# A hybrid decoder layer on one Trainium2 core: w_in's blocks scaled in place and split whole, and a memory pool for each pair's right-hand factors

## The chip, the core and the metric

The kernel runs on one core of one Trainium2 chip. The metric is the device time of one execution in microseconds. Below, PE is the matrix engine (TensorE), PEld its weight loads, DVE is VectorE, ACT is ScalarE, POOL is GpSimd, and SP is the queue that issues the DMA transfers.

## What is computed

One layer of a hybrid decoder, for 512 prompt tokens and for 8 samples of 8 tokens (576 columns together), all in fp32. Cut to what matters here:

```python
proj = rmsnorm(x, g_mix) @ w_in          # 2048 -> some 5128 columns
a, b, c, d = four mixers of 512 channels # gated DeltaNet, S5, windowed attention, RG-LRU
x = x + concat(a, b, c, d) @ w_out
x = x + cross_attention(rmsnorm(x, g_cross))
hup = rmsnorm(x, g_ffn) @ w_up           # 2048 -> 11264 columns
u, g = split(causal_conv3(hup))
x = x + (silu(g) * u) @ w_down           # 5632 -> 2048
y = rmsnorm(x, g_final)
```

The outputs are y for both groups and the new caches and states (22 arrays).

## The kernel before

Activations stand with channels on partitions: a chunk of 128 channels by 576 tokens is one tile. Every large product keeps fp32 precision by a split: a factor is cut into a part `hi`, rounded to the type fp32r, and a part `lo`, the rest, also fp32r. Three products (hi times hi, hi times lo, lo times hi) are added up in PSUM.

**Weights.** `block` (lines 114 to 130) loads one block of 512 rows by 256 columns (128 partitions by 1024 elements) into a buffer `raw` with SP, and makes `hi` and `lo` of it. There are two buffers each of `raw`, `hi` and `lo`. Without a gain it is one ACT cast of 1024 elements and one DVE subtraction of 1024 elements (lines 123 and 124). With a gain, as for w_in, whose rows are multiplied by g_mix, it is four pairs, one for each 128 rows: ACT makes hi of 256 elements with the gain as its scale (line 128), and DVE makes lo from raw, gain and hi in a fused operation (line 129). w_in has 80 such blocks. `linear` (line 132) multiplies: 48 matmuls of 288 columns for a block of 256 columns.

**Order.** A scheduler in the framework orders each engine's instructions ahead of time, by priorities that `at(...)` sets ("first", "evac", "weights", "drain", "mix", "side", "fill") and by simulated times. On the chip each engine and the SP queue take their instructions in that order, and wait on semaphores.

**Stages.** First x is transposed by PE into `xh` and `xl` (`first_x`). Then w_in's products run, mixed with the work of the four mixers, then w_out, cross-attention, the up-projection (w_up), the down-projection and the final norm.

**The up-projection.** It has 44 products of 256 columns. The first three are plain (`plain_pair`, line 497): they read the normalised rows in `xn`, four pools of four channel chunks each (hi and lo, 18,432 bytes of a partition in a pool), in the order xn0 to xn3. The other 41 (`up_pair`, line 515) use a scheme with 7 products in place of 8, after Winograd, on 2x2 cuts: each product runs over four stretches of 512 rows, and reads of w_up sums that POOL makes (`S`), and of the activations sums that `ffn_x` (line 464) makes once.

**The right factors.** `ffn_x` does this for a pair q of channel chunks (8 pairs): SP loads the pair from DRAM into `z` (line 481); DVE multiplies it by g_ffn and by the row norm r (line 483, two instructions); DVE makes two differences in `t12` (line 476, four subtractions); `halves` (lines 335 to 337) makes Bh and Bl of z, and Th and Tl of t12, each hi by an ACT cast and each lo by a DVE subtraction. Pairs 0 to 3 lie in one pool `xa`, pairs 4 to 7 in one pool `xb`; a pair takes 16,128 bytes of a partition. `xb` is opened where the four `xn` pools lay, after these are closed. A tile of a new pool waits until the pools that lay at its pool's addresses are no longer in use.

The third plain product's results leave PSUM by six DVE instructions (lines 634, 636 and 637). Below this is called the third evacuation.

Of the kernel before, what the change touches and what calls it, by code (L numbers as in the profile page):

```python
# [7 lines left out]
F32 = mybir.dt.float32  # L8
F32R = mybir.dt.float32r
AF = mybir.ActivationFunctionType  # L10
OP = mybir.AluOpType
# [3 lines left out]
NT = 576  # L15
# [3 lines left out]
class Net:  # L19
# [94 lines left out]
    def block(self, w, k0, nk, c0, ncol, gain=None):  # L114

        nc = self.nc
        with self.at("weights"):
            raw = self.wp.tile([128, nk, ncol], F32, tag="raw", name="raw", bufs=2)
            nc.sync.dma_start(raw, w[128 * k0:128 * (k0 + nk), c0:c0 + ncol].rearrange("(k p) c -> p k c", p=128))
            hi = self.wp.tile([128, nk, ncol], F32R, tag="hi", name="hi")  # L120
            lo = self.wp.tile([128, nk, ncol], F32R, tag="lo", name="lo")
            if gain is None:
                nc.scalar.copy(hi, raw)  # L123
                nc.vector.tensor_tensor(lo, raw, hi, op=OP.subtract)  # L124
            else:
                for k in range(nk):
                    g = gain[:, k0 + k:k0 + k + 1]
                    nc.scalar.activation(hi[:, k], raw[:, k], AF.Copy, scale=g)  # L128
                    nc.vector.scalar_tensor_tensor(lo[:, k], raw[:, k], g, hi[:, k], op0=OP.mult, op1=OP.subtract)  # L129
        return hi, lo  # L130

    def linear(self, xh, xl, w, c0, ncol, done, k0=0, nk=None, gain=None):
# [145 lines left out]
class Post(Net):  # L278
# [185 lines left out]
    def ffn_x(self, xc, fp, qs):  # L464

        nc, z = self.nc, {}

        for q in reversed(qs):
            for i, n in ((0, 3), (1, 4)):
                if i:  # L470

                    z[q] = xc.tile([128, 2, NT], F32, name="z", tag=f"h{q}")
                    self.X[q, 1, 1] = xc.tile([128, n, 288], F32R, name=f"Tl{q}")
                else:
                    self.X[q, 0, 0], self.X[q, 0, 1] = (xc.tile([128, n, 288], F32R, name=f"B{p}{q}") for p in "hl")
        sub = lambda o, x, y: nc.vector.tensor_tensor(o, x, y, op=OP.subtract)
        flat = lambda y: y.rearrange("p a b -> p (a b)")
        for q in qs:
            with self.at("drain"):
                x = z[q]  # L480
                nc.sync.dma_start(x, self.xd[2 * q:2 * q + 2].rearrange("k p t -> p k t"))
                for k in range(2):
                    nc.vector.scalar_tensor_tensor(x[:, k], x[:, k], self.v("g_ffn", 2 * q + k), self.r, op0=OP.mult, op1=OP.mult)
                b11, b12, b21, b22 = (x[:, k, 288 * j:288 * j + 288] for k in range(2) for j in range(2))
                t = [fp.tile([128, 592], F32, name="t12", tag=g, bufs=1)[:, :NT].rearrange("p (a b) -> p a b", a=2) for g in "ts"]
                sub(t[0][:, 0], b12, b11)
                sub(t[0][:, 1], b22, t[0][:, 0])
                sub(t[1][:, 0], b22, b12)
                sub(t[1][:, 1], t[0][:, 1], b21)
                h, l = self.X[q, 0, 0], self.X[q, 0, 1]  # L490
                self.halves(h[:, 0], l[:, 0], b11)
                self.halves(flat(h[:, 1:]), flat(l[:, 1:]), x[:, 1])
                h, l = self.X[q, 1, 0], self.X[q, 1, 1] = xc.tile([128, 4, 288], F32R, name=f"Th{q}", tag=f"h{q}"), self.X[q, 1, 1]
                for i in range(2):
                    self.halves(h[:, 2 * i:2 * i + 2], l[:, 2 * i:2 * i + 2], t[i])

# [1506 lines left out]
class Full(S5):  # L2003
# [45 lines left out]
    def run(self):  # L2049
        tc, nc = self.tc, self.nc  # L2050
        pool = lambda n, **k: tc.tile_pool(name=n, bufs=1, **k)
        R = dict(side="right")
# [3 lines left out]
        with ExitStack() as post, ExitStack() as late, ExitStack() as keep, ExitStack() as dx:  # L2056
# [54 lines left out]
            with ExitStack() as ups:  # L2111
                with ExitStack() as xns:

                    self.xn = [xns.enter_context(pool(f"xn{i}", **R)) for i in (3, 2, 1, 0)][::-1]
                    self.mean = xns.enter_context(pool("mn", **R)).tile([128, 128], F32, name="mean")
                    nc.gpsimd.memset(self.mean, 1.0 / 2048)
                    with pool("cw", **R) as cw:
                        self.banks = (0, 1)
                        with self.at("mix"):
                            self.cross_open(cw)  # L2120
                        self.w_out(2, "g_cross")
                        self.banks = (0, 1, 2, 3)
                        with self.at("mix", (3,)):
                            self.row_rstd()
                        self.cross(cw)
                    with self.at("mix", (2, 3)):
                        for m in range(16):
                            self.square(m)
                        self.row_rstd()
                    late.close()  # L2130
                    self.banks = (3,)
                    f1, fp, xa = (ups.enter_context(pool(n)) for n in ("f1", "fp", "xa"))
                    self.ffn_x(xa, fp, range(4))
                    up = self.ffn_up(fp, f1)
                    next(up)
                    for _ in range(3):
                        up.send(self.plain_pair)
                xb, sp = (ups.enter_context(pool(n, **R)) for n in ("xb", "sp"))
                self.ffn_x(xb, fp, range(4, 8))
                for i in range(3, 44):  # L2140
                    up.send(lambda w, c0, done: self.up_pair(sp, w, c0, done, (3, 2, 0, 1) if i == 43 else (0, 1, 2, 3)))
# [44 lines left out]
```

## Time and profile before

| | |
|---|---|
| median of 3 runs | 3052.51 us (3049.77 to 3057.75) |
| the profiled execution | 3051.51 us |
| its span in the trace | 3049.4 us |
| PE busy | 2906.1 us, 95% |
| PEld busy | 2743.9 us, 90% |
| DVE busy | 2074.2 us, 68% |
| ACT busy | 1134.3 us, 37% |
| POOL busy | 1054.8 us, 35% |
| mean granted TensorE clock | 0.986 of full speed |

The span is what the trace shows from the first to the last instruction; 2.1 us of the execution lie around it. A busy share is an average over all stages. PE's share is high, so a gain can only come from the time in which PE stands idle, or runs at a lower granted clock, in single stages.

### The profile page before, as it was taken

How to read it: one execution, taken by the hardware profiler on the slowest of the kernel's cores; microseconds unless marked ns; L12 is line 12 of the kernel's file. 1: busy time of each engine (PE TensorE's matmuls, PEld its weight loads, DVE VectorE, ACT ScalarE, POOL GpSimd, SP SyncE). 2: the span in 40 equal slices, each digit the busy share in tenths (PEclk: the TensorE clock that was granted, in tenths of full speed). 3: DMA queues.
4: the chain of work that ended last, by engine and by line, in shares of the span. 5: the costliest groups of instructions: out<-in, count | busy, mean ns of one | idle time of the engine just before them, and what ended most of it. 6: DMA issues, size and time to landing. Idle time of an engine off the chain costs nothing. (4 is left out here: it accounts for less than half of the span.)

```text
span 3049.4 us, 53981 instructions
## 1 busy us (share of the span) xinstructions
PE 2906.1 (95%) x21347; PEld 2743.9 (90%) x21347; DVE 2074.2 (68%) x3440; ACT 1134.3 (37%) x2025; POOL 1054.8 (35%) x1181
## 2 busy tenths in 40 slices
PE   8979988998999999998899999999999999999998
PEld 7879987887888879988899999999999999999996
DVE  7866666779567566559788888888888953333334
ACT  5434331353433353325344444444444432212214
POOL 2000322313112000102468888888878810000000
PEclk9999999999999999999999999999999999999999
DMA  5455566545566474234333333333333363323322
GB/s 162 151 160 163 173 183 194 160 131 163 168 212 185 139 217 134 80 119 149 118 96 103 107 103 109 107 109 104 107 99 107 114 202 114 104 94 114 107 90 104
DMA packets 370134, 408.41 MB, mean 134 GB/s; under 512 B 37718, under 2 KB 300716, under 8 KB 369177
## 3 DMA queue, kind: packets, MB, share of 16 engines
q1 hardware_dynamic: 369880, 404.96, 42.9%
q8 instruction: 168, 2.75, 0.4%
q14 instruction: 86, 0.70, 0.1%
HBM read 342.85 MB, written 64.69 MB: 134 GB/s over the span
## 5 line engine op out<-in xcount | busy, mean ns | idle before, releaser
L123 ACT CAST hi<-raw 128x1024 fp32r<-128x1024 f32 x158 | 165.6, 1048 | 487.7 <-PE acc L151 422.7
L151 PE MATMUL acc<-xh,hi 128*128 128x288 f32 x1408 | 319.7, 305 | 11.1 <-DVE nt L1185 10.8
L124 DVE TENSOR_TENSOR lo<-raw,hi 128x1024 fp32r<-128x1024 f32 x158 | 195.8, 1240 | 190.9 <-ACT hi L123 187.1
L151 PE MATMUL acc<-xh,lo 128*128 128x288 f32 x1408 | 316.8, 304 | 2.8 <-DVE lo L129 2.8
L151 PE MATMUL acc<-xl,hi 128*128 128x288 f32 x1408 | 319.3, 304 | 0.0
L337 DVE TENSOR_TENSOR lo<-S,hi 128x1024 fp32r<-128x1024 f32 x164 | 227.8, 1389 | 85.6 <-ACT hi L336 85.6
L151 PE MATMUL acc<-hh,hi 128*128 128x288 f32 x1280 | 275.4, 296 | 3.1 <-DVE xT L294 2.5
L337 DVE TENSOR_TENSOR al<-raw,ah 128x512 fp32r<-128x512 f32 x328 | 267.2, 850 | 15.8 <-ACT ah L336 15.8
L151 PE MATMUL acc<-hh,lo 128*128 128x288 f32 x1280 | 273.8, 295 | 1.1 <-DVE lo L124 1.1
L151 PE MATMUL acc<-hl,hi 128*128 128x288 f32 x1280 | 274.4, 295 | 0.0
L151 PEld LDWEIGHTS acc<-xh,hi 128*128 128x128 f32 x1408 | 231.7, 192 | 22.4 <-issue 17.1
L336 ACT CAST hi<-S 128x1024 fp32r<-128x1024 f32 x164 | 171.8, 1047 | 207.7 <-POOL S L532 172.3
L151 PEld LDWEIGHTS acc<-xl,hi 128*128 128x128 f32 x1408 | 232.8, 192 | 9.8 <-issue 9.1
L151 PEld LDWEIGHTS acc<-xh,lo 128*128 128x128 f32 x1408 | 231.7, 192 | 9.6 <-issue 4.4
L294 DVE TENSOR_TENSOR xT<-acc,xT 128x576 f32<-128x576 f32 x160 | 120.7, 755 | 167.1 <-PE acc L151 165.9
L529 POOL TENSOR_TENSOR S<-raw 128x256 f32<-128x256 f32 x164 | 168.3, 1026 | 152.6 <-DMA raw<-in_w_up 121.5
L128 ACT ACTIVATE hi<-raw,gmix 128x256 fp32r<-128x256 f32 x320 | 136.9, 500 | 207.1 <-PE acc L151 186.7
L151 PEld LDWEIGHTS acc<-hh,hi 128*128 128x128 f32 x1280 | 206.2, 188 | 3.9 <-ACT hi L123 2.4
L151 PEld LDWEIGHTS acc<-hh,lo 128*128 128x128 f32 x1280 | 206.4, 188 | 1.3 <-DVE lo L124 1.3
L151 PEld LDWEIGHTS acc<-hl,hi 128*128 128x128 f32 x1280 | 206.8, 188 | 0.0
L553 PE MATMUL acc<-Bh,ah 128*128 128x288 f32 x656 | 197.0, 300 | 9.8 <-ACT t L558 9.7
L627 DVE SCALAR_TENSOR_TENSOR y<-ub,vec,y 128x592 f32<-128x592 f32 x176 | 179.9, 1043 | 35.2 <-ACT y L625 34.4
(705 smaller groups left out, 8109.8 us busy)
## 6 DMA issues: line engine op xcount, KB each, us to landing
raw<-in_w_up SPq DMA_DIRECT2D x176, 512.0 KB
raw<-in_w_down SPq DMA_DIRECT2D x88, 512.0 KB
raw<-in_w_in SPq DMA_DIRECT2D x80, 512.0 KB
raw<-in_w_out SPq DMA_DIRECT2D x32, 512.0 KB
hx<-t SPq DMA_DIRECT2D x44, 288.0 KB
ht<-hx SPq DMA_DIRECT2D x44, 288.0 KB
old<-in_cache_win_k SPq DMA_DIRECT2D x48, 256.0 KB
old<-in_cache_win_v SPq DMA_DIRECT2D x48, 256.0 KB
```

Source lines behind the costliest of these rows:

```text
L123: nc.scalar.copy(hi, raw)
L124: nc.vector.tensor_tensor(lo, raw, hi, op=OP.subtract)
L128: nc.scalar.activation(hi[:, k], raw[:, k], AF.Copy, scale=g)
L151: nc.tensor.matmul(acc[m][:, 224 + 288 * j:512 + 288 * j], wt[:, k, 128 * m:128 * m + 128], at(x, kb + k)[:, 288 * j:288 * j + 288], start ...
L294: nc.vector.tensor_tensor(x, ps, old, op=OP.add)
L336: self.nc.scalar.copy(hi, src)
L337: self.nc.vector.tensor_tensor(lo, src, hi, op=OP.subtract)
L529: g(S[:, 0], A(2, 1), A(2, 2), op=OP.add)
L553: nc.tensor.matmul(P[name], wt[:, i, q], xx, start=ch == chs[0] and q == 0 and j == 0, stop=ch == chs[3] and q == 1 and j == 2)
L627: nc.vector.scalar_tensor_tensor(y, u[:, k:k + 592], w(k), y, op0=OP.mult, op1=OP.add)
```

## The change

In a block with a gain, ACT first multiplies raw by the gain in place, again by four instructions of 256 elements; then one ACT cast of 1024 elements makes hi, and one DVE subtraction of 1024 elements makes lo. For the right factors, there is one pool for each pair in place of one for four pairs, in the same order, at the same addresses.

```diff
                 for k in range(nk):
-                    g = gain[:, k0 + k:k0 + k + 1]
-                    nc.scalar.activation(hi[:, k], raw[:, k], AF.Copy, scale=g)
-                    nc.vector.scalar_tensor_tensor(lo[:, k], raw[:, k], g, hi[:, k], op0=OP.mult, op1=OP.subtract)
+                    nc.scalar.activation(raw[:, k], raw[:, k], AF.Copy, scale=gain[:, k0 + k:k0 + k + 1])
+                nc.scalar.copy(hi, raw)
+                nc.vector.tensor_tensor(lo, raw, hi, op=OP.subtract)
...
-                    z[q] = xc.tile([128, 2, NT], F32, name="z", tag=f"h{q}")
-                    self.X[q, 1, 1] = xc.tile([128, n, 288], F32R, name=f"Tl{q}")
+                    z[q] = xc[q].tile([128, 2, NT], F32, name="z", tag=f"h{q}")
+                    self.X[q, 1, 1] = xc[q].tile([128, n, 288], F32R, name=f"Tl{q}")
                 else:
-                    self.X[q, 0, 0], self.X[q, 0, 1] = (xc.tile([128, n, 288], F32R, name=f"B{p}{q}") for p in "hl")
+                    self.X[q, 0, 0], self.X[q, 0, 1] = (xc[q].tile([128, n, 288], F32R, name=f"B{p}{q}") for p in "hl")
...
-                    f1, fp, xa = (ups.enter_context(pool(n)) for n in ("f1", "fp", "xa"))
+                    f1, fp = (ups.enter_context(pool(n)) for n in ("f1", "fp"))
+
+                    xa = {q: ups.enter_context(pool(f"xa{q}")) for q in (3, 2, 1, 0)}
                     self.ffn_x(xa, fp, range(4))
...
-                xb, sp = (ups.enter_context(pool(n, **R)) for n in ("xb", "sp"))
+                xb = {q: ups.enter_context(pool(f"xb{q}", **R)) for q in (7, 6, 5, 4)}
+                sp = ups.enter_context(pool("sp", **R))
                 self.ffn_x(xb, fp, range(4, 8))
```

(The tile of Th in `ffn_x` also comes from `xc[q]`.) The scheduler places the instructions anew, and the order moves in many places of the first stages. Three places are spoken of below.

**DVE around the third evacuation.** Before, from the evacuation (L634) on; z of pair 4 is multiplied (L483) behind it:

```order
L634 TENSOR_TENSOR ub0_15373<-sq0_15163,acc_15902 128x288
L636 TENSOR_TENSOR ub0_15373<-sq0_15163,acc_15902 128x224
L637 TENSOR_TENSOR ub0_15373<-sq0_15163,acc_15902 128x8x8
L634 TENSOR_TENSOR ub1_15374<-sq0_15163,acc_15903 128x288
L636 TENSOR_TENSOR ub1_15374<-sq0_15163,acc_15903 128x224
L637 TENSOR_TENSOR ub1_15374<-sq0_15163,acc_15903 128x8x8
L337 TENSOR_TENSOR lo_16313<-S_16305,hi_16312 128x1024
L627 SCALAR_TENSOR_TENSOR y_16129<-ub0_15373,vec_1527,y_16129 128x592
L627 SCALAR_TENSOR_TENSOR y_16136<-ub1_15374,vec_1527,y_16136 128x592
L483 SCALAR_TENSOR_TENSOR z_16165<-z_16165,vec_1527,sq0_15163 128x576 x2
```

Now, up to the evacuation's first instruction (the last row here); the digit in Bl4, Tl4 and Bl5 is the pair:

```order
L476 TENSOR_TENSOR t12_16028<-z_16023,t12_16028 128x288
L337 TENSOR_TENSOR Bl4_16022<-z_16023,Bh4_16021 128x576
L337 TENSOR_TENSOR al_16169<-raw_16161,ah_16168 128x512
L476 TENSOR_TENSOR t12_16029<-t12_16028,z_16023 128x288
L337 TENSOR_TENSOR al_16169<-raw_16161,ah_16168 128x256
L337 TENSOR_TENSOR lo_16107<-S_16099,hi_16106 128x1024
L337 TENSOR_TENSOR Tl4_16024<-t12_16028,Th4_16038 128x576
L483 SCALAR_TENSOR_TENSOR z_16019<-z_16019,vec_1511,sq0_15003 128x576 x2
L337 TENSOR_TENSOR Tl4_16024<-t12_16029,Th4_16038 128x576
L476 TENSOR_TENSOR t12_16046<-z_16019 128x288
L337 TENSOR_TENSOR Bl5_16018<-z_16019,Bh5_16017 128x288
L634 TENSOR_TENSOR ub0_15222<-sq0_15003,acc_15751 128x288
```

All of pair 4's DVE instructions (two of L483, four of L476, two for Bl4, two for Tl4) and four of pair 5's (two of L483, one of L476, one for Bl5) have moved ahead of the third evacuation. None stood there before.

**The SP queue at the same place.** Before, the four loads of z behind four blocks of w_up:

```order
L524 DMA raw_16239<-in_w_up 128x4x256
L659 DMA hx1_15329<-t_15898 128x576
L524 DMA raw_16303<-in_w_up 128x4x256
L524 DMA raw_16362<-in_w_up 128x4x256
L524 DMA raw_16421<-in_w_up 128x4x256
L481 DMA z_16165<-xd_81 128x2x576
L481 DMA z_16161<-xd_81 128x2x576
L481 DMA z_16157<-xd_81 128x2x576
L481 DMA z_16153<-xd_81 128x2x576
```

Now:

```order
L524 DMA raw_16097<-in_w_up 128x4x256
L659 DMA hx1_15178<-t_15747 128x576
L481 DMA z_16023<-xd_81 128x2x576
L524 DMA raw_16161<-in_w_up 128x4x256
L524 DMA raw_16220<-in_w_up 128x4x256
L481 DMA z_16019<-xd_81 128x2x576
L524 DMA raw_16279<-in_w_up 128x4x256
L481 DMA z_16015<-xd_81 128x2x576
L481 DMA z_16011<-xd_81 128x2x576
```

The load of pair 4 has moved ahead of three blocks of w_up, and that of pair 5 ahead of one.

**ACT at the start**, where it casts the transposed x (L244), squares it (L251), and makes the first two blocks of w_in. Before:

```order
L1359 ACTIVATE dal<-dal 128x4
L244 CAST xh<-pm 128x4x128
L1337 CAST wbs<-wb 128x16x8
L244 CAST xh<-pm 128x4x64
L251 ACTIVATE nj,nss<-nx 64x1024
L244 CAST xh<-pm 128x4x64 x2
L251 ACTIVATE nj,nss<-nx 64x1024
L244 CAST xh<-pm 128x4x64
```

Now:

```order
L1359 ACTIVATE dal<-dal 128x4
L244 CAST xh<-pm 128x4x128
L1337 CAST wbs<-wb 128x16x8
L244 CAST xh<-pm 128x4x64
L128 CAST hi<-raw 128x1024
L251 ACTIVATE nj,nss<-nx 64x1024
L244 CAST xh<-pm 128x4x64
L128 CAST hi<-raw 128x1024
L244 CAST xh<-pm 128x4x64 x2
L251 ACTIVATE nj,nss<-nx 64x1024
```

The two new casts of w_in's blocks stand ahead of the last casts of x, and one square has moved behind them. The scaling instructions of these blocks stand where line 128's stood.

## Rows read from the trace of the kernel before

**Rows 1.** Busy time by stage: window, its length, each engine's busy us (instructions), clock, DMA.

```profile
0.00:840.00 840.00, 765.95 (x5856) 699.44 (x5857) 587.13 (x1278) 314.40 (x679) 183.77 (x204) 0.97 0.55 164
...
1545.00:2450.00 905.00, 890.69 (x6639) 881.35 (x6639) 774.36 (x1064) 398.89 (x650) 755.55 (x860) 1.00 0.34 107
```

**Rows 2.** What PE waited for, 0 to 840 us: total, times, longest.

```profile
PE acc L151 <- DVE nt L1185: 10.8, 4, 7.5
...
PE pm L1472 <- DVE dw L1466: 4.5, 1, 4.5
...
PE pm L865 <- DVE nt L275: 4.2, 1, 4.2
...
PE acc L151 <- DVE lo L129: 2.8, 3, 1.2
```

**Rows 3.** Busy time in windows of 10 us, order as in rows 1.

```profile
1500.00:1510.00 10.00, 5.12 (x36) 4.60 (x35) 10.00 (x15) 4.52 (x9) 5.01 (x6) 0.92 0.30 104
1510.00:1520.00 10.00, 6.32 (x30) 5.95 (x29) 10.00 (x15) 2.75 (x5) 5.99 (x5) 0.56 0.17 52
1520.00:1530.00 10.00, 7.96 (x42) 6.98 (x40) 8.61 (x15) 4.37 (x7) 4.41 (x4) 0.83 0.11 29
1530.00:1540.00 10.00, 6.43 (x31) 5.42 (x30) 7.76 (x13) 3.10 (x5) 3.36 (x4) 0.83 0.08 26
```

**Rows 4.** What PE waited for, 1500 to 1540 us.

```profile
PE acc L553 <- DVE Bl L337: 5.6, 2, 3.7
PE pp L553 <- ACT Th L336: 4.2, 2, 3.0
PE pp L553 <- DVE Bl L337: 3.0, 1, 3.0
```

**Rows 5.** Timelines of PE, SP and DVE, 1483 to 1498 us: start, us, instruction.

```profile
1492.23 0.42 PE L508 MATMUL acc<-xh,lo 128*128 128x288 f32 x2
...
1492.87 1.99 SPq L481 DMA_DIRECT2D z<-xd  x4
...
1488.52 1.58 DVE L337 TENSOR_TENSOR al<-raw,ah 128x512 fp32r<-128x512 f32 x2 [4.78 <-ACT ah L336]
...
1497.47 1.54 DVE L483 SCALAR_TENSOR_TENSOR z<-z,vec,sq 128x576 f32<-128x576 f32 x2
```

**Rows 6.** Groups, 0 to 840 us: busy us, mean ns, idle before.

```profile
L129 DVE SCALAR_TENSOR_TENSOR lo<-raw,gmix,hi 128x256 fp32r<-128x256 f32 x320 | 171.2, 576 | 38.0 <-ACT hi L128 34.0 <-DMA ys<-Y 3.1
...
L128 ACT ACTIVATE hi<-raw,gmix 128x256 fp32r<-128x256 f32 x320 | 136.9, 500 | 207.1 <-PE acc L151 186.7 <-issue 9.3 <-DMA raw<-in_w_in 7.2
```

**Rows 7.** Groups of the whole span: whole-block casts and subtractions.

```profile
L123 ACT CAST hi<-raw 128x1024 fp32r<-128x1024 f32 x158 | 165.6, 1048 | 487.7 <-PE acc L151 422.7
...
L124 DVE TENSOR_TENSOR lo<-raw,hi 128x1024 fp32r<-128x1024 f32 x158 | 195.8, 1240 | 190.9 <-ACT hi L123 187.1
...
L337 DVE TENSOR_TENSOR lo<-S,hi 128x1024 fp32r<-128x1024 f32 x164 | 227.8, 1389 | 85.6 <-ACT hi L336 85.6
```

**Rows 8.** Waits of all engines, 0 to 840 us.

```profile
ACT hi L128 <- PE acc L151: 186.7, 48, 13.9
...
DVE lo L129 <- ACT hi L128: 34.0, 21, 4.8
```

**Rows 9.** The start: busy time of 20 to 30 us, and ACT's timeline.

```profile
20.00:30.00 10.00, 6.47 (x36) 5.18 (x35) 8.43 (x21) 9.98 (x25) 0.00 (x0) 0.67 0.40 106
...
26.42 1.11 ACT L251 ACTIVATE nj<-nx 64x1024 f32<-64x1024 f32 x1
```

**Rows 10.** DVE's groups from 1491.9 to 1537 us.

```profile
L483 DVE SCALAR_TENSOR_TENSOR z<-z,vec,sq 128x576 f32<-128x576 f32 x8 | 7.6, 987 | 0.1
L337 DVE TENSOR_TENSOR Tl<-t,Th 128x576 fp32r<-128x576 f32 x8 | 6.6, 860 | 1.2 <-ACT Th L336 1.2
...
L476 DVE TENSOR_TENSOR t<-z 128x288 f32<-128x288 f32 x8 | 4.4, 583 | 0.0
L337 DVE TENSOR_TENSOR Bl<-z,Bh 128x576 fp32r<-128x576 f32 x4 | 3.0, 746 | 0.0
```

More of the change, by code (lines that the diff above doesn't have):

```diff
@@ L492, in ffn_x @@
                 self.halves(flat(h[:, 1:]), flat(l[:, 1:]), x[:, 1])
-                h, l = self.X[q, 1, 0], self.X[q, 1, 1] = xc.tile([128, 4, 288], F32R, name=f"Th{q}", tag=f"h{q}"), self.X[q, 1, 1]
+                h, l = self.X[q, 1, 0], self.X[q, 1, 1] = xc[q].tile([128, 4, 288], F32R, name=f"Th{q}", tag=f"h{q}"), self.X[q, 1, 1]
                 for i in range(2):
```

## The prediction

> **What bounds the kernel now.** I read the busy time by stage first, then PE's waits in the two stages that the change touches, then 10-us windows and timelines. PE does nearly all it can: from 1545 to 2450 us it is busy for 890.69 of 905 us, 6639 matmuls at 890.69 / 6639 = 0.134 us each [rows 1]. So the change can only act where PE is idle or slow. Two such places count. From 0 to 840 us, where w_in's blocks run among the mixers' work, PE is busy for 766 of 840 us, 74 us less than the window; DVE works 587 us there, ACT 314 [rows 1]. The waits in that stage are scattered: the largest that end with DVE are 10.8, 4.5 and 4.2 us, and only 2.8 us are waits for a lo of w_in itself [rows 2]. The second place is sharp. In the four windows from 1500 to 1540 us PE issues 36 + 30 + 42 + 31 = 139 matmuls [rows 3], where 40 / 0.134 = 298 would fit: 159 are lacking, 21 us. DVE is busy for all of the first two windows [rows 3], and PE's waits name it and the casts that it feeds: Bl 5.6 and 3.0 us, Th 4.2 us [rows 4]. The reader should see a late start behind this: the last plain matmuls begin at 1492.23, the four loads of z go out from 1492.87 on, the first product with z starts on DVE at 1497.47 [rows 5]. One pool held all four pairs, and so waited for all of `xn`.
>
> **The pools (change at 1480 to 1540 us).** From the tile sizes, pairs 7, 6, 5, 4 lie one on the other, 16,128 bytes each, over xn3, xn2, xn1, xn0 of 18,432 each. So pair 4 (bytes 48,384 to 64,512) lies over xn1 and xn0, pair 5 over xn2 and xn1, pairs 6 and 7 over xn3. A plain product reads xn0 first, and spends 48 matmuls, 48 x 0.134 = 6.4 us, on each pool. Counted back from 1492.5, xn1 is free at about 1479.7 and xn2 at 1486.1. The load then takes as long as before, 1497.47 - 1492.87 = 4.6 us [rows 5], so z of pair 4 is there at about 1484.3 and that of pair 5 at about 1490.7; pairs 6 and 7 gain nothing. SP has the loads in places that fit, but the queue is in order: a z that waits for its pool holds up the block of w_up behind it.
>
> What moves ahead of the third evacuation on DVE: four of L483 at 0.99, 3.9 us; five of L476 at 0.58, 2.9 us; one wide Bl at 0.75 and two narrow ones, taken at 0.58 like L476 of the same 288 elements, 1.9 us; two Tl at 0.86, 1.7 us [rows 10]. Together 10.4 us. If all of it fell into empty DVE time, the end of the factors would come 10.4 us sooner. But DVE's empty time between 1484.3 and the evacuation is mostly one gap of 4.78 us that ends at 1488.52 [rows 5]; the rest pushes the evacuation back, which PE covers for a while with matmuls into other PSUM banks. I take the middle of 4.8 and 10.4, **7.5 us**. PE also ran slowly there: from 1510 to 1520 us the granted clock is 0.56, a mix of the 1.2 and 2.4 GHz levels, after the waits for Bl, and 30 matmuls took 6.32 us in which 47 fit at 0.134 [rows 3]. That is 2.3 us; with shorter waits I take back **1.5**. For `xa` I take nothing: its factors wait for the row norm r, which is made later than the old tiles are free, and their first use is some 50 us later behind three plain products. If that cover were gone, the 21 us of the second place would be the price again.
>
> **The blocks of w_in (0 to 840 us).** DVE drops 320 fused operations, 171.2 us busy, one every 576 ns [rows 6], and gets 80 subtractions. That exact operation stands in the trace at 1240 ns, and in the stage where POOL is busiest at 1389 ns [rows 7]; 80 x 1.24 = 99 us is my value, since POOL is less busy here, and 111 us the upper end. DVE loses 72 us of 587, 12%. I let the DVE waits of PE shrink in the same share: 10.8 + 4.5 + 4.2 + 2.8 = 22.3 us [rows 2], 12% of it **3 us**. Bounds: nothing, and half of the 22.3, 11 us.
>
> The Trainium skill's page "VectorE: DVE Perf Modes" (section on the TRN2 errata) gives an fp32 tensor_tensor (N + 151) / 0.96 ns, so 1224 ns at 1024 elements, which agrees with 1240, and 424 at 256. By that estimate four small operations against a large one save 80 x (4 x 424 - 1224) = 38 us, not 72, and the term would be 1.4 us in place of 3. The trace's 576 ns is above it, and the measurement decides.
>
> ACT keeps 320 scalings. In place and with an fp32 result they are not in the trace; the nearest row, the same instruction with an fp32r result, has 500 ns [rows 6], and I take it unchanged. Bounds: 100 ns less or more each, 32 us of ACT busy time either way. It gets 80 casts at 1048 ns [rows 7], 84 us on top of 314, so 398 of 840 us: no bound by load. The path matters more. In 48 of 80 blocks ACT waited at line 128 for PE to give back a hi buffer, 186.7 us [rows 8]. The scaling writes raw, so it no longer waits for that, and goes into this wait; then cast and subtraction take 1.05 + 1.24 = 2.3 us, what four overlapped pairs took (four scalings of 0.43 us pitch, 136.9 / 320, and one DVE operation of 0.58, also 2.3 us). So for these blocks lo is ready, raw is free and SP is released as before: nothing. In the other 32 the cast adds 1.05 us; PE has 48 x 0.134 = 6.4 us of the previous block to cover it, so I take nothing, and keep 32 x 1.05 = 34 us as the upper end.
>
> At the start there is no cover. ACT is busy for 9.98 of 10 us from 20 to 30 us [rows 9], PE waits for x, and two casts of 1.05 us now stand ahead of the last casts of x, while one square of 1.11 us [rows 9] has gone behind them: **1 us lost**.
>
> **The sum.** -7.5 - 1.5 - 3 + 1 = -11 us. The profiled execution of 3051.5 us (span 3049.4 and 2.1 around it) becomes 3040.5. That execution was 1.0 us under the median of 3052.5, so I expect a median of **3041.5 us**. About 0.3%, 9.2 us, is what a measurement of this kernel can tell from no change, so a time under 3043.3 is faster; my value is just beyond. The first 1100 us are scheduled anew everywhere, which can shift PE's small waits by some us either way.
>
> **Rivals.**
> 1. *The loads of z stay late.* If pair 4 waits for its pool behind other SP work, or DVE's new order only changes which of two saturated stretches does the work, the second place keeps its 21 us. For: DVE is busy throughout [rows 3], and the total of its work is the same. Against: the gap of 4.78 us is there. Time: 3052.5 - 3 + 1 = 3050.5. Chance 0.20.
> 2. *ACT becomes the late link in w_in, slower.* The cast stands in ACT's in-order queue between other work, so hi comes 1.05 us later in the 32 blocks for which ACT did not wait. It decides from the point where hi is later than the 6.4 us that the previous block covers, so wherever other late work stands in front of the cast. All of them late: 3052.5 + 34 - 9 + 1 = 3078.5. For: DVE already waited 34 us for these hi [rows 8]. Against: PE's own waits for lo of w_in are 2.8 us [rows 2]. Chance 0.15. The Trainium skill's page "ScalarE: Activation LUTs" (rules for kernel authors) tells to put additions and multiplications on VectorE; it speaks against more ScalarE work, but here DVE is the fuller engine, 587 against 314 us [rows 1].
> 3. *The second stall goes entirely, and DVE's waits halve.* 3052.5 - 21 - 11 + 1 = 3021.5. For: once the factors come in time, the slow clock goes too. Against: pairs 6 and 7 are as late as before. Chance 0.13.
>
> **How the numbers follow.** The forecast has the remaining 0.52, with a range of its own of 3032 to 3051: 0.36 of it is faster by over 0.3%, 0.16 within. Faster: 0.36 + 0.13 = 0.49. Within 0.3%: 0.16 from the forecast and 0.16 from rival 1, 0.32. Slower: 0.15 from rival 2 and 0.04 from a new schedule with worse waits in rival 1, 0.19. The range of 8 in 10 goes from 3021, the third rival, to 3064, which takes in half of rival 2's delay.
>
> **What would show it.** Right: the load of pair 4 goes out some 13 us before the last plain matmul, not after it; DVE has no gap of 4.78 us before the third evacuation; the four windows hold some 60 to 70 matmuls more, and a stall that names pairs 6 and 7 remains. From 0 to 840 us DVE's busy time falls by about 70 us and ACT's rises by about 84, and PE's waits with DVE shrink by a few us. Wrong: the loads of z still stand together behind the last plain product; or PE's waits for hi or lo of w_in, 2.8 us now, grow to tens of us; or ACT's in-place scaling takes much more than 500 ns.

## The result and the profile after

The changed kernel takes 3080.2 us, the median of four runs from 3072.11 to 3084.63, against 3052.7 for the kernel before, measured four times beside it: a ratio of 1.0079 with a 95% interval of 1.0063 to 1.0095, so some 24 us slower. The forecast was 3041.5 us and a range up to 3064. The number is near that of rival 2, 3078.5, but the runs below show that rival 2's mechanism carries at most some third of it.

The profiled execution of after is the fastest of the four: 3072.11 us, span 3070.3, which is 20.9 us more than before. PE's 21347 matmuls took 2921.7 us in place of 2906.1, DVE worked 2018.5 us (2074.2 before), ACT 1207.7 (1134.3), and the mean granted clock fell from 0.986 to 0.979.

The first view is the busy time by window, with columns as in [rows 1].

```profile
0.00:840.00 840.00, 762.79 (x5740) 695.59 (x5741) 518.66 (x1017) 383.26 (x751) 180.76 (x199) 0.95 0.54 161
1545.00:2450.00 905.00, 886.96 (x6575) 876.96 (x6576) 771.54 (x1064) 397.61 (x649) 757.79 (x862) 0.99 0.33 105
1500.00:1510.00 10.00, 10.00 (x77) 10.00 (x77) 6.18 (x10) 2.91 (x6) 4.17 (x5) 1.00 0.68 204
1510.00:1520.00 10.00, 8.11 (x59) 7.64 (x58) 10.00 (x13) 4.26 (x8) 7.33 (x7) 1.00 0.62 223
1520.00:1530.00 10.00, 8.09 (x59) 7.89 (x60) 10.00 (x17) 5.78 (x10) 6.47 (x9) 1.00 0.14 53
1530.00:1540.00 10.00, 7.44 (x49) 6.30 (x49) 10.00 (x16) 4.14 (x9) 6.52 (x3) 1.00 0.21 61
```

Up to 840 us PE has issued 5740 matmuls where it had issued 5856 [rows 1]: at 0.134 us each, 15.5 us are already gone, though DVE is busy for 68 us less than before. From 1500 to 1540 us it issued 244 where [rows 3] have 139, but that is another piece of the program now, since everything comes later; this is sorted out under e1.

The operations themselves cost what was forecast. These are the groups of w_in's blocks, 0 to 840 us, as in [rows 6].

```profile
L127 ACT ACTIVATE raw<-raw,gmix 128x256 f32<-128x256 f32 x320 | 137.4, 500 | 267.7 <-DMA raw<-in_w_in 251.4 <-DVE rt L1924 8.9 <-DVE nt L1195 7.1
L129 DVE TENSOR_TENSOR lo<-raw,hi 128x1024 fp32r<-128x1024 f32 x79 | 105.7, 1338 | 88.7 <-ACT hi L128 88.2 <-PE acc L151 0.2
L128 ACT CAST hi<-raw 128x1024 fp32r<-128x1024 f32 x79 | 82.4, 1043 | 50.7 <-PE acc L151 50.6
```

The in-place scaling takes 500 ns, the cast 1043, the subtraction 1338 (1240 was taken, 1389 was the upper end). These windows end before the last of the 80 blocks (x79), as the work has moved back. What stands behind the bar is new. Here are the waits of ACT and DVE, 0 to 840 us, with the columns of [rows 8].

```profile
ACT raw L127 <- DMA raw<-in_w_in: 251.4, 67, 12.5
ACT hi L128 <- PE acc L151: 50.6, 27, 6.1
...
DVE lo L129 <- ACT hi L128: 88.2, 38, 8.7
```

ACT's 186.7 us of waiting for PE at line 128 [rows 8] have become 50.6, and 251.4 us of waiting for raw's transfer have come, where the hi's of before had waited 7.2 us for it [rows 6]. DVE's wait for hi went from 34.0 [rows 8] to 88.2 us. PE's own waits with DVE hardly moved, as its view for 0 to 840 us shows (compare [rows 2]). Its wait for a lo of w_in rose only from 2.8 to 6.2 us, so the sign that the prediction named for a late ACT, tens of us, did not appear:

```profile
PE acc L151 <- DVE lo L129: 6.2, 3, 3.4
...
PE pm L1472 <- DVE dw L1466: 4.7, 2, 2.8
PE acc L151 <- DVE nt L1185: 4.4, 1, 4.4
PE pm L865 <- DVE nt L877: 4.1, 1, 4.1
```

### The profile page after: what moved, and what is told of

Its sections match the earlier page's. It is cut to its first block, busy times and chain, and to the rows that moved or that the text cites. A ratio compares the mean times of both kernels' runs of the same rounds, so it can differ in the third digit from the quotient of the medians.

```text
span 3070.3 us, 53839 instructions
## 1 busy us (share of the span) xinstructions
PE 2921.7 (95%) x21347; PEld 2755.4 (90%) x21347; DVE 2018.5 (66%) x3200; ACT 1207.7 (39%) x2105; POOL 1066.9 (35%) x1181
## 5 line engine op out<-in xcount | busy, mean ns | idle before, releaser
L127 ACT ACTIVATE raw<-raw,gmix 128x256 f32<-128x256 f32 x320 | 137.4, 500 | 267.7 <-DMA raw<-in_w_in 251.4
L553 PE MATMUL acc<-Bh,ah 128*128 128x288 f32 x656 | 197.0, 300 | 15.5 <-ACT t L558 14.0
L529 POOL TENSOR_TENSOR S<-raw 128x256 f32<-128x256 f32 x164 | 161.0, 982 | 132.1 <-DMA raw<-in_w_up 103.3
L553 PE MATMUL pp<-Th,hi 128*128 128x288 f32 x656 | 195.5, 300 | 7.7 <-DVE u L563 3.7
```

The lines of the kernel that those rows point to most:

```text
L127: nc.scalar.activation(raw[:, k], raw[:, k], AF.Copy, scale=gain[:, k0 + k:k0 + k + 1])
L529: g(S[:, 0], A(2, 1), A(2, 2), op=OP.add)
L553: nc.tensor.matmul(P[name], wt[:, i, q], xx, start=ch == chs[0] and q == 0 and j == 0, stop=ch == chs[3] and q == 1 and j == 2)
```

## The experiments

All numbers are ratios to the kernel before on the same chip, with their 95% intervals; 0.001 is 3.06 us.

| run | what | ratio | interval |
|---|---|---|---|
| e1 | the pools alone | 1.0017 | 1.0006 to 1.0028 |
| e2 | the scaling alone | 1.0078 | 1.0065 to 1.0091 |
| e3 | same work, four hi's written ahead of four lo's | 1.0003 | 0.9993 to 1.0014 |
| e4 | the change, GpSimd scales | 1.0006 | 0.9995 to 1.0017 |
| e12 | scaling alone, GpSimd scales | 1.0005 | 0.9992 to 1.0017 |
| e8 | scaling alone, DVE scales | 1.0106 | 1.0088 to 1.0125 |
| e5 | before, with an early touch of raw on ACT | 1.0026 | 1.0014 to 1.0039 |
| e6 | before, with 70 us of idle ACT work | 1.0061 | 1.0043 to 1.0078 |
| e7 | scaling alone, held until PE returns hi | 1.0033 | 1.0019 to 1.0047 |
| e9 | touch and idle work together | 1.0040 | 1.0026 to 1.0054 |
| e10 | twice the idle work | 1.0010 | 0.9998 to 1.0021 |
| e11 | a third of the idle work | 1.0044 | 1.0027 to 1.0062 |
| e13 | scaling, all in the order of before | 1.0029 | 1.0015 to 1.0044 |
| e14 | the same, ACT alone free | 1.0120 | 1.0106 to 1.0134 |
| e15 | old work in the scaling's order | 0.9997 | 0.9988 to 1.0006 |
| e16 | idle work in the order of before | 1.0017 | 1.0006 to 1.0028 |
| e17 | old work and the touch, in the order of e14 | 1.0072 | 1.0057 to 1.0087 |
| e18 | old work in the order of e10 | 1.0010 | 1.0001 to 1.0020 |

### One part at a time: e1 to e4

**e1, e2.** Each takes one part of the diff and leaves the other as before.

> Only the pools for each pair; w_in's blocks as before. First theory (the loss comes from the blocks of w_in; the pools give what the trace of the change shows, 22.8 us behind when the plain products end and 20.3 us behind when the up-projection ends, so some 2.5 us, perhaps up to the 9 us forecast): 3044 to 3050 us. Rival (the pools only move the stall, since SP and DVE are in order, and cost as much as they give): 3050 to 3056 us.

> Only the scaling in place with whole casts; one pool for four pairs. First theory (the blocks of w_in cost about 24 us before 1270 us, and the pools give 2 to 9 us): 3076 to 3090 us. Rival (the loss needs both parts, for instance by the order that the scheduler finds for both): under 3065 us.

The scaling alone gives the whole loss, 1.0078. The pools give none of it back; they cost 2 to 9 us themselves, and e1's median of 3060.0 us lies above both expectations. Yet the loads came ahead as forecast. These are SP's, PE's and DVE's timelines of after (start, us, instruction), and the third evacuation in before:

```profile
1502.69 0.37 SPq L481 DMA_DIRECT2D z<-xd  x1
...
1509.09 0.37 SPq L481 DMA_DIRECT2D z<-xd  x1
...
1515.85 0.97 SPq L481 DMA_DIRECT2D z<-xd  x2
...
1515.03 0.43 PE L508 MATMUL acc<-xh,lo 128*128 128x288 f32 x2
...
1508.03 1.66 DVE L483 SCALAR_TENSOR_TENSOR z<-z,vec,sq 128x576 f32<-128x576 f32 x2 [1.10 <-DMA z<-xd]
...
1521.95 0.44 DVE L634 TENSOR_TENSOR ub<-sq,acc 128x288 f32<-128x288 f32 x1
```

```profile
1491.90 0.46 DVE L634 TENSOR_TENSOR ub<-sq,acc 128x288 f32<-128x288 f32 x1
```

The first z goes out 12.3 us before the last plain matmul at 1515.03 (13 forecast), the second 5.9 us before it. But the third evacuation, at line 634, now comes 6.9 us after that matmul; before it came 0.3 us ahead of it, at 1491.90 against 1492.23. To compare the same place, take 60 us from the last plain matmul on, first whole, then the first 10, the next 10 and the 20 behind them, of before and then of after (columns as in [rows 1]).

```profile
1492.23:1552.23 60.00, 45.83 (x284) 42.95 (x283) 55.33 (x84) 26.33 (x43) 32.51 (x37) 0.86 0.29 98
1492.23:1502.23 10.00, 10.00 (x78) 10.00 (x77) 9.85 (x14) 6.24 (x10) 9.84 (x13) 1.00 0.78 290
1502.23:1512.23 10.00, 3.67 (x21) 2.80 (x19) 10.00 (x15) 3.90 (x8) 5.08 (x6) 0.81 0.17 57
1512.23:1532.23 20.00, 15.10 (x73) 13.39 (x73) 18.61 (x30) 6.54 (x11) 9.08 (x8) 0.75 0.17 52
```

```profile
1515.03:1575.03 60.00, 45.86 (x289) 42.55 (x288) 52.03 (x77) 25.73 (x42) 39.02 (x39) 0.89 0.27 87
1515.03:1525.03 10.00, 6.20 (x43) 5.54 (x42) 10.00 (x18) 4.89 (x7) 6.24 (x8) 1.00 0.48 170
1525.03:1535.03 10.00, 8.26 (x63) 7.97 (x62) 10.00 (x12) 7.12 (x13) 6.06 (x5) 1.00 0.01 2
1535.03:1555.03 20.00, 13.10 (x67) 11.43 (x66) 15.19 (x23) 3.52 (x6) 18.44 (x14) 0.74 0.26 81
```

284 matmuls against 289: 5 x 0.134 = 0.7 us. The stall has not shrunk, it has moved. In before PE ran on for 10 us behind the plain product (78 matmuls) and then fell to 21; in after it falls at once, to 43, and has 63 in the next ten. DVE is full in these 20 us as before. The 20 us behind them hold 67 matmuls where they held 73, and there DVE is no longer the full engine, POOL is (18.44 of 20 us, 9.08 before). PE's waits, from 1480 to 1570 us in after, name other releasers than the factors of [rows 4]; of these 2.4 us for hi, and 0.6 for the evacuation itself, lie in the first 10 us:

```profile
PE acc L553 <- ACT t L558: 5.2, 1, 5.2
PE pp L553 <- ACT hi L336: 2.4, 1, 2.4
PE acc L553 <- DVE al L337: 1.9, 2, 1.7
```

e1's own trace has the same picture: the evacuation 6.7 us behind the last plain matmul, then 38 and 69 matmuls in the first two stretches of 10 us, 290 in 60 us.

**e3** writes the four hi's of a block first and the four lo's after them, meant as a control for a new order.

```diff
-                    nc.scalar.activation(hi[:, k], raw[:, k], AF.Copy, scale=g)
-                    nc.vector.scalar_tensor_tensor(lo[:, k], raw[:, k], g, hi[:, k], op0=OP.mult, op1=OP.subtract)
+                    nc.scalar.activation(hi[:, k], raw[:, k], AF.Copy, scale=gain[:, k0 + k:k0 + k + 1])
+                for k in range(nk):
+                    nc.vector.scalar_tensor_tensor(lo[:, k], raw[:, k], gain[:, k0 + k:k0 + k + 1], hi[:, k], op0=OP.mult, op1=OP.subtract)
```

> The kernel before with the same eight instructions for a block of w_in, but written as four scalings and then four fused operations, so that the scheduler may order them another way; no work is changed. If the loss is ACT's queue held up by the new scaling, which waits for the transfer of raw: within 6 us of before, 3047 to 3059 us. Rival (any new order of the first stages costs or gains some 20 us by chance): 15 us or more away from before, either way.

1.0003, but it tested nothing: in its trace PE's 21347 matmuls and DVE's 3440 instructions stand in exactly the order of before. The question of the order stayed open until e15.

**e4** is the change with GpSimd in ACT's place for the scaling.

```diff
-                    nc.scalar.activation(raw[:, k], raw[:, k], AF.Copy, scale=gain[:, k0 + k:k0 + k + 1])
+                    nc.gpsimd.tensor_scalar(raw[:, k], raw[:, k], gain[:, k0 + k:k0 + k + 1], None, op0=OP.mult)
```

> The change, but GpSimd scales raw in place in place of ACT; ACT makes only the cast, DVE the one subtraction. If the loss is that the scaling waits for raw's transfer in ACT's queue (251 us, 67 waits) and holds up ACT's other work: the wait goes to GpSimd's queue, ACT's busy time falls by 137 us, and the time is 3040 to 3060 us. Rival (the long chain from raw to hi, with a whole cast behind the scaling, makes hi late): the chain is no shorter, GpSimd's scalings are slower than ACT's, and the time is 3080 us or more.

1.0006: the loss is gone with the scaling off ACT. But with it went both ACT's load and ACT's wait for raw, so e4 does not say which of them it was.

### Load, early wait, longer way: e5 to e12

Three theories stood here. Theory 1: the scaling needs nothing but raw's transfer, so the scheduler puts it early in ACT's order; there it waits, and ACT's other work waits behind it. Theory 2: ACT simply has too much to do. Theory 3: the way from raw to hi and lo has become longer.

**e5** adds an early wait without work, **e6** work without an early wait, **e7** makes the scaling wait for PE's release of hi first, **e8** moves it to DVE.

```diff
+                nc.scalar.copy(raw[:, :, :1], raw[:, :, :1])
                 for k in range(nk):
                     g = gain[:, k0 + k:k0 + k + 1]
```

> The kernel before, with one more ACT instruction per w_in block: a copy of one column of raw's four sub-blocks onto itself, ahead of the hi's. Like the in-place scaling it needs only raw's transfer, not PE's release of hi, so it stands as early in ACT's order; it adds 80 short operations (estimate from the smallest ACT operations of the trace, 0.2 us each: 16 us of ACT). Theory 1 (ACT's in-order queue is held by an instruction that waits for raw's transfer): most of the +24 us of the scaling alone comes back, 3068 to 3082 us against 3056. Theory 2 (ACT's additional load of about 84 us makes it late): a fifth of the load, +0 to +5 us. Theory 3 (the chain from raw through the scaling to hi and lo is longer): the hi's are as before and the chain is 0.2 us longer, +0 to +5 us.

```diff
+                for k in range(3):
+                    idle = self.wp.tile([128, 128], mybir.dt.bfloat16, tag="idle", name="idle", bufs=1)
+                    nc.scalar.copy(idle, hi[:, k, :128])
```

> The kernel before, with three more ACT copies per w_in block that read 128 columns of hi into a scratch tile nobody reads; they stand behind the hi's and wait for nothing that hi does not. Estimate of their load: some 0.35 us each, 240 of them, 84 us, the amount that the scaling added. Theory 1: +0 to +6 us, since nothing new waits for a transfer. Theory 2: +15 to +30 us. Theory 3: +0 to +6 us, the way from raw to hi and lo is unchanged.

```diff
+                nc.scalar.copy(hi[:, :, :1], raw[:, :, :1])
                 for k in range(nk):
                     nc.scalar.activation(raw[:, k], raw[:, k], AF.Copy, scale=gain[:, k0 + k:k0 + k + 1])
```

> The scaling alone (pools as before), but held until PE has returned hi: ACT first copies one column of raw's sub-blocks into hi (0.2 us), and the in-place scaling, which overwrites that column of raw, comes after it. ACT's load is that of the scaling alone and 16 us more, the way from the release of hi to hi and lo is longer by the scaling (4 x 0.5 us), and nothing waits for raw's transfer earlier than the hi's did before. Theory 1: most of the loss goes, 3054 to 3066 us. Theory 2: it stays, 3076 to 3090 us. Theory 3: it grows, since 2 us stand between the release of hi and the cast in each block that PE waits for: 3085 to 3120 us.

```diff
-                    nc.scalar.activation(raw[:, k], raw[:, k], AF.Copy, scale=gain[:, k0 + k:k0 + k + 1])
+                    nc.vector.tensor_scalar(raw[:, k], raw[:, k], gain[:, k0 + k:k0 + k + 1], None, op0=OP.mult)
```

> Pools as before; DVE instead of ACT scales raw in place (four operations per block), ACT casts once, DVE subtracts once. ACT's load falls by a third of the hi's, DVE's rises by 320 in-place scalings, by some 0.3 to 0.5 us each 100 to 160 us (estimate from DVE's four subtractions with gain, whose one pass over 256 columns took about as long). Theory 1: the early wait for raw's transfer moves into DVE's queue, which feeds more work than ACT's, so slower than the scaling alone, 3075 to 3110 us. Theory 2: ACT is relieved, 3050 to 3062 us, unless DVE, which is the busier engine, becomes the bound. Theory 3: like theory 1 in sign but smaller, +5 to +20 us.

e7 and e8 went as theory 1 has it: held, the scaling costs 10 us in place of 24, on DVE 32. Against it, e5's touch waited 269.7 us for raw and cost only 8, and e6's idle copies cost 18.5 us, as theory 2 has it. So I varied the idle work (**e9**: three copies and the touch; **e10**: six copies; **e11**: one) and tried GpSimd's scaling without the new pools (**e12**, e4's line in e2).

> The kernel before with both additions at once: the one-column copy that waits early for raw's transfer, and the three copies per block that only take ACT's time. Theory A (the two burdens, an early wait in ACT's in-order queue and more ACT work, add up, and the scaling's own result is their sum less what DVE saves): 1.0026 - 1 and 1.0061 - 1 give 8 + 18 = 26 us, 3074 to 3090 us against 3056, a little over the scaling alone, which also relieves DVE. Theory B (each result is chance: any other order of the same work lands somewhere within 20 us): 3050 to 3076 us, not above the larger of the two by more than a few us.

> Six of the idle copies per block in place of three: by the trace of three (240 copies of 294 ns) 141 us of ACT's time in place of 70.5. Theory A, load: about twice the +18.5 us, 3082 to 3100 us. Theory B, chance: no relation to the load, anywhere from 3050 to 3076 us.

> One idle copy per block: 80 x 0.294 = 23.5 us of ACT's time. Theory A, load: a third of the +18.5 us, +3 to +9 us, 3059 to 3065 us. Theory B, chance: anywhere from 3050 to 3076 us.

> Pools as before; GpSimd scales raw in place, ACT casts once per block, DVE subtracts once. With the pools of the change this measured 1.0006, and the pools alone 1.0017. Theory A: ACT has 137 - 84 = 53 us less to do and DVE 72 us less, and the early wait for raw's transfer is GpSimd's, which feeds less work; less the pools' 5 us it gives 3044 to 3056 us, the best of all. Theory B: within 6 us of the kernel before on either side.

Theory 2 fell here. One copy cost 13 us, three 18.5, six 3, though six take the most time, as the groups of e6 and then of e10 show (0 to 860 us):

```profile
L132 ACT CAST idle<-hi 128x128 bf16<-128x128 f32 x240 | 70.5, 294 | 3.6
```

```profile
L132 ACT CAST idle<-hi 128x128 bf16<-128x128 f32 x480 | 142.0, 296 | 10.3
```

Nor did touch and copies add up. What these runs have in common is that each edit made the scheduler lay out the first stages anew, some little and some nearly whole. Compared by tiles and shapes, of PE's first 9000 matmuls 41% stand in e6 at the place that they had before, 40% in e2, 44% in e10, 65% in e11, and 92% in e5. So the order had to be held fixed.

### The order held fixed: e13 to e18

These kernels carry a list of the wanted order of each engine, and tie each instruction behind its neighbour on its engine; such a tie fixes the order of issue and waits for nothing.

```diff
+        for x, y in zip(order, order[1:]):
+            tc.add_manual_dep(lists[e][y], lists[e][x].name,
+                              mybir.DependencyInfo(mybir.DependencyClass.NoSync, mybir.DependencyReason.DATA), reason="order")
```

**e13** is e2 with the list of before, **e14** the same without ACT's list, **e15** the kernel before with e2's lists, **e16** e6 with the lists of before for PE, DVE and ACT. Theory A is now the order, B the early wait, C the longer way to hi and lo.

> The scaling alone, with the instructions of PE, DVE, GpSimd, SP and ACT held to the order of the kernel before by issue-order edges (no waits): the four scalings and the cast stand where the fourth hi stood, the one subtraction where the fourth lo stood. Theory A (order): the loss goes, 3045 to 3060 us against 3055.5. Theory B (early wait for raw in ACT's queue): the loss goes as well, since the scalings stand behind what the hi's stood behind. Theory C (the longer way to hi and lo): it stays, 3075 us or more.

> As the scaling in the order of before, but ACT's order is left to the scheduler, which puts the scalings early again, ahead of other ACT work; PE, DVE, GpSimd and SP stay as in the kernel before. Theory A: near e13, within 6 us, 3045 to 3062 us. Theory B: the early wait costs by itself, most of the 24 us returns, 3070 to 3082 us.

> The arithmetic of the kernel before (hi's with the gain, four subtractions, nothing in place), with PE, DVE, GpSimd, SP and ACT held to the order that the scaling alone got; the hi's stand where the cast stood, the lo's where the one subtraction stood, and nothing waits early for raw in ACT's queue. Theory A: slower without any scaling, 3066 to 3082 us. Theory B or C: as before, 3052 to 3060 us.

> The kernel before with the three idle ACT copies per block (70.5 us of ACT), PE, DVE and ACT held to the order of before, the copies right behind the hi's. Theory A: of the 18.5 us that the copies cost in the scheduler's own order little is left, 3052 to 3062 us. Load: 3070 to 3078 us.

e15 says that the scaling's order is as good as the old one, 0.9997: theory A falls for e2. e16 leaves 5 of e6's 18.5 us, so most of that was order. e13 says that in the order of before the new work costs 1.0029, 9 us, a little more than A and B had expected. And e14 says what the place in ACT's queue does: every other engine is in the order of before. By the two traces ACT's other work is in its old order but for 19 instructions moved by at most four places, and 76 of the 80 casts stand where they stood. What differs is the scalings: in 65 of 80 blocks they stand further ahead, in half of all by three or more instructions of other work. 1.0120 comes out, 28 us more than e13 and above what B had expected. ACT's waits, 0 to 840 us, in e13 and then in e14:

```profile
ACT hi L128 <- PE acc L151: 117.0, 41, 14.8
...
ACT raw L127 <- DMA raw<-in_w_in: 20.4, 10, 5.9
```

```profile
ACT raw L127 <- DMA raw<-in_w_in: 216.3, 63, 8.6
ACT hi L128 <- PE acc L151: 71.9, 30, 6.2
```

One place in e14 shows the whole chain; SP's, ACT's and PE's timelines, 86 to 96 us:

```profile
86.35 0.39 SPq L119 DMA_DIRECT2D raw<-in_w_in  x1
...
91.69 1.70 ACT L127 ACTIVATE raw<-raw,gmix 128x256 f32<-128x256 f32 x4 [8.47 <-DMA raw<-in_w_in]
93.30 0.24 ACT L1788 COPY kw<-pm 128x128 f32<-128x128 f32 x1
...
87.39 0.42 PE L151 MATMUL acc<-xl,hi 128*128 128x288 f32 x2
87.65 0.43 PE L151 MATMUL acc<-xh,lo 128*128 128x288 f32 x2
93.59 0.48 PE L1790 MATMUL pm<-ident,kw 128*128 128x128 f32 x1 [5.51 <-ACT kw L1788]
...
95.25 0.68 PE L151 MATMUL acc<-xh,lo 128*128 128x288 f32 x2
95.73 0.68 PE L151 MATMUL acc<-xh,hi 128*128 128x288 f32 x2
```

The transfer of raw goes out at 86.35 and lands 5.3 us later. The scaling stands at ACT's head for 8.47 us, and behind it the short copy of kw, whose input PE made before 85 us. PE needs kw next in its order, and sits 5.51 us. In before the copy at this place of the order ran as soon as PE was done:

```profile
78.41 0.27 ACT L1788 COPY kw<-pm 128x128 f32<-128x128 f32 x1 [4.10 <-PE pm L1785]
```

Added up over the rows of PE's waits from 0 to 1300 us that end with ACT, it is 8.3 us before, 15.5 in e13 and 34.1 in e14; in after, with the scheduler's own layout, it is 16.7. These are e14's largest:

```profile
PE acc L151 <- ACT hi L128: 7.6, 3, 6.0
...
PE pm L1877 <- ACT ut L1874: 5.7, 2, 5.1
PE pm L1056 <- ACT kt L1052: 5.7, 6, 2.0
PE pm L1268 <- ACT nt L1269: 5.5, 2, 5.4
PE pm L1790 <- ACT kw L1788: 5.5, 1, 5.5
```

Four of these five are other work than w_in's; the second alone is as large in before, 6.3.

**e17** puts e5's touch where e14 has its first scaling, the four hi's where it has the cast, on the old work; **e18** is the kernel before in the order of e10.

> The one-column copy in place of the scaling, every engine held: PE, DVE, GpSimd and SP in the order of the kernel before, ACT in the order that it had in e14 (the copy where the first scaling stood, the four hi's where the cast stood). Theory B (the early wait for raw's transfer by itself): most of the 27 us that e14 lies above e13 is here too, 3070 to 3082 us against 3055.5. Theory B' (the wait hurts only with the scaling's 1.7 us between raw's landing and whatever ACT does next): 3055 to 3066 us.

> The arithmetic of the kernel before, all engines held to the order that the scheduler found with six idle copies per block, which are left out again. With them it took 3.2 us over the kernel before (1.0010); three of them in the order of before cost 4.7 us, so six some 9. Theory A (the order is worth what is left): 3045 to 3054 us, a version that beats both. If the order of before is no worse than this one: 3055 to 3063 us.

e17 shows that the early wait is enough: one column copied onto itself, 201 ns each, with no scaling, a way only that much longer and the old DVE work, costs 1.0072, 22 us, by where it stands and what it waits for. PE's waits that end with ACT, 0 to 1300 us, are 20.5 us here. The touch's own wait, 0 to 840 us:

```profile
ACT raw L126 <- DMA raw<-in_w_in: 251.1, 66, 11.6
```

Why the same touch cost only 8 us in e5 is not shown. It stands about as far ahead there, in 64 of 80 blocks, and waits as long, and PE's order is for the most part the old one. That the scheduler had laid out the rest around the touch is likely, but no run tests it. So the price of an early wait depends on the layout, 8 us in one and 22 to 28 in the other. e18 gives 1.0010, the same as e10 with its 142 us of idle work. No version that beats the kernel before came out of these runs; those with GpSimd, e4 and e12, and e15 equal it.

## Why the prediction was wrong

- **The step that failed** is the one on the path of w_in's blocks: "The scaling writes raw, so it no longer waits for that, and goes into this wait", priced at nothing. It took the time in which ACT had waited for PE as free. But ACT takes its instructions in an order that is fixed beforehand: in the place above a copy whose input was there before 85 us ran at 93.30, behind the scaling. The scaling did not slip into the old wait; it stood at the head of the queue and brought a wait of its own, for raw's transfer (7.2 to 251.4 us), with other ACT work behind it. With the other engines in the order of before this costs 22 us (e17) to 28 us (e14 less e13). In the scheduler's layout the scaling as a whole costs 24 (e2); that order by itself costs nothing (e15) and the same work behind the old waits 9 (e13), so some 15 are left for the early wait there, an estimate that no run measures by itself. The trace of before had the clue: raw has two buffers, its load waited 124.4 us in 35 places for lo to be done, and ACT waited for PE, not for raw, only because PE's release came later still.
- **Rival 2** had the in-order queue but the wrong instruction. It feared the cast, and hi 1.05 us later, +34 us if all 32 blocks were late. That work in the old order is e13, 9 us, and with the scheduler's order and the scaling held back e7, 10. That its time came so near is chance.
- **The DVE term, 3 us**: the cause was right but smaller. From 0 to 840 us DVE's work fell from 587 to 519 us, but less of the program lies in that window now; over the whole span DVE's operations for w_in fell from 171.2 to 107.0 us, and DVE as a whole by 55.7 (72 forecast). The effect was not seen: PE's waits that end with DVE, 0 to 1300 us, add up to 48.2 us before and 47.9 after. DVE's own waits for hi grew by 54.2 us in the same stage.
- **The pools, 7.5 and 1.5 us**: the loads came ahead as worked out, 12.3 us against 13. The gain of 7.5 was taken between bounds of 4.8 and 10.4; 0.7 us was there. What failed is "the rest pushes the evacuation back, which PE covers for a while": the evacuation went back 7.2 us, and PE covered little of it: it issued 43 matmuls in place of 78 in the 10 us behind the plain product, and what was won in the next ten did little more than make that good. ACT's t and hi are the largest releasers now. This is rival 1: DVE's new order only changed what is late. The 1.5 us for the clock, which hung on shorter waits, are not to be seen apart from the 0.7.
- **Sizes** were right: scaling 500 ns, cast 1043, subtraction 1338 between 1240 and 1389. One reading was not: 576 ns is how long a fused operation takes, and 171.2 / 320 = 535 ns is how often one came; no term hangs on it.
- **The range** ended at 3064 because rival 2 was counted half. The remark that the first 1100 us are scheduled anew, "some us either way", was too small as well: e6's copies cost 18.5 us in the scheduler's order and 5 in the old one, so the order alone was worth some 13 us there, give or take 6, and nothing in e15.

What stays open: why e13 itself costs 9 us. Its longer way to hi and lo would explain it, but GpSimd's scaling, which is on the same way, costs nothing (e12), though in another layout and with less work on ACT; nothing was run that parts these. Open too is which of PE's waits in after brought its clock down (below).

## What to carry to other kernels

In an in-order queue ask of every moved or added instruction which semaphore it waits for, and what stands behind it: an operation that waits for a transfer can cost the queue its wait, however short it is (201 ns here), and an engine at 37% load can still hold up one at 95%. Where a scheduler lays out the program, an edit is two changes, the work and the order; fix the order to see the first alone. The stall behind a saturated engine stayed here when that engine's work was only reordered: something else was late next.

## What the runs showed of the hardware

PE ran slower behind a long wait. At the place in e14 the granted clock is 1.00 from 80.00 to 87.50 us, and 0.53, mostly the lower of the two levels (1.2 and 2.4 GHz), from 93.60 to 97.00, after PE had stood for 5.51 us (columns as in [rows 1]):

```profile
80.00:87.50 7.50, 7.50 (x65) 6.82 (x64) 3.36 (x4) 2.83 (x7) 7.19 (x8) 1.00 0.12 43
93.60:97.00 3.40, 3.40 (x15) 3.40 (x16) 1.45 (x2) 0.88 (x1) 0.00 (x0) 0.53 0.06 8
```

In the timelines above, rows of two matmuls each begin 0.26 us apart before the wait (87.39 to 87.65) and 0.48 behind it (95.25 to 95.73). So part of a loss stands in PE's busy time, and in after it is the larger part: of 20.9 us of span, 15.6 are longer busy time for the same 21347 matmuls, while PE's waits from 0 to 1300 us grew only from 85.9 to 92.4 us and the granted clock from 0 to 840 us fell from 0.97 [rows 1] to 0.95. There is no fixed price for a wait: in e14 PE's busy time takes 19.9 us of a span 41.8 longer, in e17 7.1 of 22.1, though there the waits to 1300 us grew by 15.8.

And 142 us of idle ACT work, in a stage where ACT worked 314 of 840 us [rows 1], made no difference that could be measured in its own order (e10 and e18, both 1.0010). In the order of before half as much, 70.5 us, cost 2 to 9 us (e16, 1.0006 to 1.0028).
